# Attention projections ahead of HGRN2, in pairs, by seven products of half depth, and x kept split in DRAM

## The chip, the cores and the metric

The kernel runs on one core of one Trainium2 chip. The metric is device time in microseconds (us) of one execution, as a median of several runs. PE (TensorE) multiplies matrices, DVE (VectorE), ACT (ScalarE) and POOL (GpSimd) work on rows, and SP (SyncE) issues every DMA of this kernel, in one queue.

## The reference

One layer mixes two kinds of heads. The input (4096 rows, 1024 columns, float32) is normalised and projected to 4096 columns; half of them feed eight attention heads with three dilations, half feed four heads of a gated recurrence (HGRN2). Both results are normalised per head, gated, and projected back.

```python
hn = _rmsnorm(x, mix_norm_w[layer])
proj = hn @ w_in[layer]
aq, ak, av, ag, hq, hf, hi, hg = jnp.split(proj, split_at, axis=-1)
aq, ak = rotary(aq), rotary(ak)
attn = _longnet_mixture(bhse(aq), bhse(ak), bhse(av))
f = lb + (1.0 - lb) * jax.nn.sigmoid(hf.astype(f32))
rec = _hgrn2_chunked(silu(hq), 1.0 - f, hi, jnp.log(f))
y_attn = _head_rmsnorm(attn, attn_out_norm_w[layer], ATTN_HEADS) * silu(ag)
y_hgrn = _head_rmsnorm(rec, hgrn_out_norm_w[layer], HGRN_HEADS) * silu(hg)
x = x + jnp.concatenate([y_attn, y_hgrn], axis=-1) @ w_out[layer]
return _rmsnorm(x, final_norm_w)
```

## The kernel before

The 4096 projected columns are eight groups of 512: A0 to A3 (q, k, v and gate of two attention heads each) and H0 to H3 (one HGRN2 head each). The rows are 32 blocks of 128. Every float32 operand of a projection is split into a high part (rounded to float32r) and a low rest, so each of the eight depth steps of 128 takes three matmuls: high by high (L195), high by low (L196), low by high (L197). One block of one group is 24 matmuls of 128x512 in `project`.

The program has four stages. First, A0 to A2 are projected block by block, and `attn_rows` (L273) turns each product into rotated, transposed and split q and k (to `qk_d`), v (`v_d`) and the gate (`sg_d`), all in DRAM. Second, A3 is projected alone (L705 on). Third come the four HGRN2 groups, in 16 pairs of blocks: `load_pair` (L200) loads four raw tiles of x from xP (256 KB each) and splits them (ACT L209, POOL L210), `project_T` and `project_N` make 96 matmuls of 128x256 (L220), and `hgrn_gates`, `hgrn_values` and `hgrn_block` do the recurrence. Fourth come the output projection and the last norm (L751 on).

Attention itself is a generator in `queue`; after each block of stages two and three `take` draws as many of its steps as `rate` gives. It starts in stage two, at block `HOLD`, so it runs beside 155 blocks. Its scores, flips and weighted sums use PE, DVE and ACT; its q, k and v come by DMA (`load_qk` L406, `vh` L534 and L539).

Weights come by `load_w` (L161): 256 KB of raw weights, then the high part on ACT (L171) and the low part on DVE (L172), into eight `whi` and eight `wlo` tiles. From A3 on, raw weights and raw x share a pool of three `raw` tiles. The order on each engine is fixed when the program is built, by the framework's scheduler from the program order, priorities and its own estimates; each engine then runs its list in order, and SP too issues its DMAs in order, each after the semaphores it waits on.

```python
rate = NH * HEAD_COST / (5 * NB - HOLD)
...
            if b >= HOLD:
                left = take(left + rate)
```

Of the kernel before, what the change touches and what calls it, by code (L numbers as in the profile page):

```python
# [49 lines left out]
def layer(ctx: ExitStack, tc: tile.TileContext, x, xT, xP, pos, w_in, w_out, nw, anw, hnw, lbraw, fnw,  # L50
# [40 lines left out]
    def rotary_tables():  # L91
        su = p1p
        pt = su.tile([128, NB], I32, name="pt", bufs=1)
        pf = su.tile([128, NB], F32, name="pf", bufs=1)
# [19 lines left out]
        A.activation(rsin, ang, AF.Sin)  # L114
        A.activation(rcos, kk, AF.Sin)
# [45 lines left out]
    def load_w(g, wp, n, rp, tag, bufs, raws=()):  # L161
        for k in range(KT):
            raw = raws[k] if k < len(raws) else fetch_w(g, k, rp, tag, bufs)
            hi = wp.tile([128, 512], F32R, name="whi", bufs=n)
            lo = wp.tile([128, 512], F32R, name="wlo", bufs=n)
            if ORDER[g][0] == "H":
                parts = ((slice(0, 128), nnwt), (slice(128, 512), nwt))
            else:
                parts = ((slice(0, 512), nwt),)
            for c, s in parts:  # L170
                A.activation(hi[:, c], raw[:, c], AF.Copy, scale=s[:, k : k + 1])  # L171
                V.scalar_tensor_tensor(lo[:, c], raw[:, c], s[:, k : k + 1], hi[:, c].bitcast(F32),  # L172
                                       op0=ALU.mult, op1=ALU.subtract)
            yield hi, lo

    def load_x(b, lo_eng):
        res = []
        with tc.high_priority():
            for h in range(2):
                raw = xp.tile([128, 512], F32, name="raw", bufs=3)  # L180
                dma(raw, xT[b, :, h * 512 : (h + 1) * 512])
                hi = xp.tile([128, 512], F32R, name="xhi", bufs=4)
                lo = xp.tile([128, 512], F32R, name="xlo", bufs=4)
                A.activation(hi, raw, AF.Copy)  # L184
                lo_eng.tensor_tensor(lo, raw, hi.bitcast(F32), op=ALU.subtract)  # L185
                res.append((hi, lo))
        return res
# [12 lines left out]
    def load_pair(t):  # L200

        res = []
        with tc.high_priority():
            for q in range(4):
                raw = xp.tile([128, 512], F32, name="raw", bufs=3)
                dma(raw, xP[t, :, q * 512 : (q + 1) * 512])
                hi = xp.tile([128, 512], F32R, name="xhi", bufs=4)
                lo = xp.tile([128, 512], F32R, name="xlo", bufs=4)
                A.activation(hi, raw, AF.Copy)  # L209
                G.tensor_tensor(lo, raw, hi.bitcast(F32), op=ALU.subtract)  # L210
# [666 lines left out]
```

## Time and profile before

| | before |
|---|---|
| median of 3 runs | 2761.05 us (2759.09 to 2762.15) |
| profiled execution | 2761.07 us |
| its span | 2759.3 us |
| mean granted TensorE clock | 0.983 |
| PE busy | 2662.0 us (96%) |
| DVE, ACT, POOL busy | 1813.9, 1749.5, 997.0 us |
| DMA | 387.95 MB, mean 141 GB/s |

Busy time is the sum of an engine's instructions in the profiled execution; the span runs from its first to its last instruction. Stages lie at about 0 to 600 us (A0 to A2), 600 to 840 (A3), 840 to 2440 (HGRN2) and 2440 to the end.

### The profile page before, as it was taken

The numbers are of one execution on the slowest core, as the hardware profiler recorded it, in microseconds if no ns is written. First come the engines' busy times: TensorE is split into PE (matmuls) and PEld (weight loads), VectorE is DVE, ScalarE is ACT, GpSimd is POOL, SyncE is SP. The second block draws the span as 40 slices with busy tenths as digits, with TensorE's granted clock in tenths as the row PEclk, the third lists the DMA queues.
The fourth block names the chain that finished last, engine by engine and source line by source line (L and its number), as shares of the span: only waits on it lengthen the run. The fifth ranks groups of instructions, "written<-read, shape, count | busy, mean of one in ns | idle before, by whom it ended". The sixth has DMA issues, their size and how long they took to land.

```text
span 2759.3 us, 54301 instructions
## 1 busy us (share of the span) xinstructions
PE 2662.0 (96%) x17714; PEld 2392.6 (87%) x17714; DVE 1813.9 (66%) x5636; ACT 1749.5 (63%) x5174; POOL 997.0 (36%) x1034
## 2 busy tenths in 40 slices
PE   7999999999998999989999999999899999999998
PEld 5888888877888999988999999999899998888887
DVE  5444444445777778777778888878877878843343
ACT  6444444446766886876887787787787788422222
POOL 2222222234445535525535535544534643200000
PEclk9999999999999999989999999999999999999999
DMA  6444444476467345336435446435435533644442
GB/s 218 144 140 141 140 141 141 138 206 191 144 189 202 93 131 161 104 108 171 113 111 161 117 120 172 126 97 157 135 100 157 146 92 99 190 139 132 136 131 87
DMA packets 450189, 387.95 MB, mean 141 GB/s; under 512 B 119112, under 2 KB 342644, under 8 KB 449908
## 3 DMA queue, kind: packets, MB, share of 16 engines
q1 hardware_dynamic: 449908, 384.50, 49.3%
q8 instruction: 141, 2.31, 0.3%
q14 instruction: 140, 1.15, 0.1%
HBM read 291.53 MB, written 92.82 MB: 139 GB/s over the span
## 4 chain that ended last, share of the span: by engine, by line
PE 78%; DVE 9%; DMA 5%; ACT 4%; issue 2%; SPq 1%; POOL 1%; DVEq 0%; POOLq 0%; ACTq 0%
PE proj L220 20%; PE proj L197 12%; PE proj L195 12%; PE proj L196 12%; PE po L466 6%; PE att L454 5%; PE att L431 3%; PE att L432 3%; PE hp L369 1%; PE hp L769 1%; DVE hgv L394 1%; PE hp L373 1%; PE hp L375 1%; PE hp L380 1%; DMA wraw<-w_in 1%
## 5 line engine op out<-in xcount | busy, mean ns | idle before, releaser
L195 PE MATMUL proj<-whi,xhi 128*128 128x512 f32 x1280 | 511.4, 400 | 18.4 <-ACT rt L276 7.7
L197 PE MATMUL proj<-whi,xlo 128*128 128x512 f32 x1280 | 514.8, 402 | 0.0
L196 PE MATMUL proj<-wlo,xhi 128*128 128x512 f32 x1280 | 511.3, 399 | 0.9 <-DVE wlo L172 0.9
L210 POOL TENSOR_TENSOR xlo<-raw,xhi 128x512 fp32r<-128x512 f32 x256 | 342.6, 1343 | 229.9 <-ACT xhi L209 196.8
L442 DVE CUSTOM_DVE_ANT_0 pt<-att,mask 128x256 f32<-128x256 f32 (+1 forms) x768 | 270.3, 388 | 94.2 <-PE att L432 91.1
L220 PE MATMUL proj<-xhi,whi 128*128 128x256 f32 x1024 | 301.8, 295 | 5.7 <-DVE hz L328 2.2
L195 PEld LDWEIGHTS proj<-whi,xhi 128*128 128x128 f32 x1280 | 243.2, 190 | 70.8 <-ACT rt L276 9.6
L220 PE MATMUL proj<-xhi,wlo 128*128 128x256 f32 x1024 | 301.5, 294 | 1.6 <-DVE wlo L172 1.5
L220 PE MATMUL proj<-xlo,whi 128*128 128x256 f32 x1024 | 301.4, 294 | 0.0
L220 PE MATMUL proj<-whi,xlo 128*128 128x256 f32 x1024 | 297.9, 291 | 0.0
L220 PE MATMUL proj<-whi,xhi 128*128 128x256 f32 x1024 | 297.5, 290 | 0.3 <-ACT hgv L355 0.3
L220 PE MATMUL proj<-wlo,xhi 128*128 128x256 f32 x1024 | 296.8, 290 | 0.0
L196 PEld LDWEIGHTS proj<-wlo,xhi 128*128 128x128 f32 x1280 | 242.6, 190 | 54.6 <-DVE wlo L172 3.0
L197 PEld LDWEIGHTS proj<-whi,xlo 128*128 128x128 f32 x1280 | 242.7, 190 | 48.8
L458 DVE TENSOR_TENSOR pl<-att,ph 128x512 fp32r<-128x512 f32 (+1 forms) x384 | 238.9, 625 | 50.3 <-ACT ph L457 48.2
L444 ACT ACTIVATE pt<-pt,ml 128x256 f32<-128x256 f32 (+1 forms) x512 | 238.2, 467 | 49.1 <-DVE ml L442 47.7
L185 POOL TENSOR_TENSOR xlo<-raw,xhi 128x512 fp32r<-128x512 f32 x126 | 162.6, 1292 | 212.4 <-ACT xhi L184 188.3
L281 DVE SCALAR_TENSOR_TENSOR rot<-rt,rsin 128x32 f32<-128x32 f32 x128 | 56.5, 442 | 276.0 <-ACT rt L276 276.0
L457 ACT ACTIVATE ph<-att 128x512 fp32r<-128x512 f32 (+1 forms) x384 | 207.5, 543 | 37.6 <-PE att L454 32.0
L454 PE MATMUL att<-ident,pt 128*128 128x128 f32 x1368 | 224.7, 278 | 3.1 <-DVE nat L442 1.2
L466 PE MATMUL po<-ph,vh 128*128 128x128 f32 (+1 forms) x856 | 217.0, 278 | 9.0 <-DVE OA L552 3.5
L466 PE MATMUL po<-pl,vh 128*128 128x128 f32 (+1 forms) x856 | 212.3, 290 | 2.8 <-DVE pl L458 2.3
(210 smaller groups left out, 7228.8 us busy)
## 6 DMA issues: line engine op xcount, KB each, us to landing
raw<-xP SPq DMA_DIRECT2D x256, 256.0 KB
raw<-xT SPq DMA_DIRECT2D x128, 256.0 KB
qk_d<-stk SPq DMA_DIRECT2D x128, 256.0 KB
vh<-v_d SPq DMA_DIRECT2D x512, 64.0 KB
raw<-x SPq DMA_DIRECT2D x64, 256.0 KB
v_d<-hl SPq DMA_DIRECT2D x128, 128.0 KB
vh<-v_d SPq DMA_DIRECT2D x64, 256.0 KB
raw<-y_d SPq DMA_DIRECT2D x64, 256.0 KB
```

The costliest lines, as they stand in the source:

```text
L185: lo_eng.tensor_tensor(lo, raw, hi.bitcast(F32), op=ALU.subtract)
L195: T.matmul(ps, hi[:, c], whi, start=(k == 0), stop=False)
L196: T.matmul(ps, hi[:, c], wlo, start=False, stop=False)
L197: T.matmul(ps, lo[:, c], whi, start=False, stop=(k == KT - 1))
L210: G.tensor_tensor(lo, raw, hi.bitcast(F32), op=ALU.subtract)
L220: m = T.matmul(o, l, r, start=first is None, stop=(k == KT - 1 and g == len(groups) - 1 and n == 2))
L442: V.tensor_tensor_reduce(out=p_, in0=o, in1=mask[:, (1, 4, 16).index(d), 256 - 128 * nk : 256], scale=-0.125, scalar=3e38, op0=ALU.add, op ...
L444: A.activation(p_, p_, AF.Exp, scale=-1.0, bias=m, accum_out=l)
L454: T.transpose(ps[:, n * 128 : (n + 1) * 128], loc[u], ident)
L457: A.activation(ph[:, :w], ps[:, :w], AF.Copy)
L458: V.tensor_sub(pl[:, :w], ps[:, :w], ph[:, :w].bitcast(F32))
L466: T.matmul(po[:, 128 * c : 128 * (c + n)], v, rh, start=(s == 0), stop=(s == len(steps) - 1))
```

## The change

A0 to A3 are all projected before HGRN2, in two pairs of groups (P = 0: A0 and A1; P = 1: A2 and A3), and in units of two blocks. For a unit the product is seen as a 2x2 matrix of 2x2: rows of two blocks (first index of A), depth in two halves (second index of A, first of B), columns of two groups (second index of B). Instead of eight products of half depth, seven are made (Winograd's form of Strassen's scheme): A11·B11, S2·T2, A12·B21, S1·T1, S3·T3, S4·B22, A22·T4, where the S are sums of parts of x and the T sums of parts of the weights. Each product is 12 matmuls of 128x512 (`half`). A12·B21 is accumulated in the bank of A11·B11, and A22·T4 in that of S3·T3; `unit_rows` adds the rest on DVE.

`summed_w` makes the sums of the weights once a pair: for each of four depth steps, four raw tiles, scaled on ACT and DVE, four sums on POOL (L675, L677, L680, L683 of the changed kernel), and five splits into `tw` tiles. `load_unit` does the like for x: four tiles from xT, sums on POOL (L698, L700, L706) and DVE, seven splits (`split_tile`; ACT for the high part, L170, and DVE or POOL for the low one, L171). `attn_rows` now handles two groups of a block at once.

Attention no longer runs beside A3: its generator is drawn beside the 128 blocks of HGRN2 alone. Split x of HGRN2 is written to DRAM (`xh_d`, 512 KB a tile) by the first HGRN2 group (L197); the other three groups load it back (L200) instead of loading and splitting raw x.

```diff
+    xh_d = [dram.tile([4, 128, 1024], F32, name=f"xh_d{t}") for t in range(NB // 2)]
...
-    def load_pair(t):
+    def load_pair(t, g):
 
         res = []
         with tc.high_priority():
             for q in range(4):
-                raw = xp.tile([128, 512], F32, name="raw", bufs=3)
-                dma(raw, xP[t, :, q * 512 : (q + 1) * 512])
-                hi = xp.tile([128, 512], F32R, name="xhi", bufs=4)
-                lo = xp.tile([128, 512], F32R, name="xlo", bufs=4)
-                A.activation(hi, raw, AF.Copy)
-                G.tensor_tensor(lo, raw, hi.bitcast(F32), op=ALU.subtract)
-                res.append((hi, lo))
+                if g == 4:
+                    raw = xp.tile([128, 512], F32, name="raw", bufs=3)
+                    dma(raw, xP[t, :, q * 512 : (q + 1) * 512])
+                    xs = split_tile(raw, G, xp, "xs", 4)
+                    dma(xh_d[t][q], xs.bitcast(F32))
+                else:
+                    xs = xp.tile([128, 1024], F32R, name="xs", bufs=4)
+                    dma(xs.bitcast(F32), xh_d[t][q])
+                res.append(parts(xs))
...
+    psq = ExitStack()
+    ps_m = psq.enter_context(tc.tile_pool(name="ps_m", bufs=5, space=PSUM))
+    ps_x = psq.enter_context(tc.tile_pool(name="ps_x", bufs=3, space=PSUM))
+    w1 = one.enter_context(tc.tile_pool(name="w1", bufs=20))
+
+    def plain_w(P, j):
+
+        res = []
+        for k in range(4):
+            raw = fetch_w(2 * P, 4 * j + k, xp, "raw", 3)
+            hi = wp.tile([128, 512], F32R, name="whi", bufs=8)
+            lo = wp.tile([128, 512], F32R, name="wlo", bufs=8)
+            s = nwt[:, 4 * j + k : 4 * j + k + 1]
+            A.activation(hi, raw, AF.Copy, scale=s)
+            V.scalar_tensor_tensor(lo, raw, s, hi.bitcast(F32), op0=ALU.mult, op1=ALU.subtract)
+            res.append((hi, lo))
+        return res
+
+    def summed_w(P, W):
+        W.update({n: [None] * 4 for n in ("T1", "T2", "T3", "T4", "B22")})
+        for k in range(4):
+            B = {}
+            for j, n in ((0, 1), (0, 0), (1, 1), (1, 0)):
+                r = B[j, n] = fetch_w(2 * P + n, 4 * j + k, p1p, "xr", 5)
+                s = nwt[:, 4 * j + k : 4 * j + k + 1]
+                if n:
+                    A.activation(r, r, AF.Copy, scale=s)
+                else:
+                    V.tensor_scalar(r, r, s, None, op0=ALU.mult)
+
+            def unit(name, src, eng):
+                W[name][k] = parts(split_tile(src, eng, w1, "tw", 20))
+
+            t1 = p1p.tile([128, 512], F32, name="tmp", bufs=2)
+            G.tensor_tensor(t1, B[0, 1], B[0, 0], op=ALU.subtract)
+            t2 = p1p.tile([128, 512], F32, name="tmp", bufs=2)
+            G.tensor_tensor(t2, B[1, 1], t1, op=ALU.subtract)
+            unit("T2", t2, V)
+            unit("T1", t1, V)
+            G.tensor_tensor(B[0, 1], B[1, 1], B[0, 1], op=ALU.subtract)
+            unit("T3", B[0, 1], V)
+            unit("B22", B[1, 1], V)
+            G.tensor_tensor(B[1, 0], B[1, 0], t2, op=ALU.subtract)
+            unit("T4", B[1, 0], V)
+
+    def load_unit(t):
+
+        a, X = {}, {}
+        for i, j in ((0, 0), (1, 0), (1, 1), (0, 1)):
+            a[i, j] = p1p.tile([128, 512], F32, name="xr", bufs=5)
+            dma(a[i, j], xT[2 * t + i, :, j * 512 : (j + 1) * 512])
+
+        def split(name, src, eng):
+            X[name] = parts(split_tile(src, eng, *((p1p, "ss", 4) if name[0] == "S" else (xp, "xs", 4))))
+
+        split("A11", a[0, 0], V)
+        s1 = p1p.tile([128, 512], F32, name="tmp", bufs=2)
+        G.tensor_tensor(s1, a[1, 1], a[1, 0], op=ALU.add)
+        s2 = p1p.tile([128, 512], F32, name="tmp", bufs=2)
+        G.tensor_tensor(s2, s1, a[0, 0], op=ALU.subtract)
+        split("S2", s2, V)
+        split("A12", a[0, 1], G)
+        split("S1", s1, G)
+        V.tensor_tensor(a[1, 0], a[0, 0], a[1, 0], op=ALU.subtract)
+        split("S3", a[1, 0], G)
+        G.tensor_tensor(s2, a[0, 1], s2, op=ALU.subtract)
+        split("S4", s2, G)
+        split("A22", a[1, 1], G)
+        return X
+
+    def half(ps, X, W, start=True):
+        for k in range(4):
+            c = slice(k * 128, (k + 1) * 128)
+            (hi, lo), (whi, wlo) = X, W[k]
+            T.matmul(ps, hi[:, c], whi, start=start and k == 0, stop=False, skip_group_check=not start)
+            T.matmul(ps, hi[:, c], wlo, start=False, stop=False, skip_group_check=not start)
+            T.matmul(ps, lo[:, c], whi, start=False, stop=(k == 3), skip_group_check=not start)
+
+    def first_product(X, W):
+        pa = ps_m.tile([128, 512], F32, name="m")
+        half(pa, X["A11"], W["B11"])
+        u2 = p1p.tile([128, 512], F32, name="u2", bufs=1)
+        A.activation(u2, pa, AF.Copy)
+        return pa, u2
+
+    def unit_rows(P, t, X, W, gv, begun):
+        pa, u2 = begun
+        b0, b1 = 2 * t, 2 * t + 1
+        C0 = p1p.tile([128, 2, 512], F32, name="C", bufs=3)
+        C1 = p1p.tile([128, 2, 512], F32, name="C", bufs=3)
+        pb = ps_m.tile([128, 512], F32, name="m")
+        half(pb, X["S2"], W["T2"])
+        V.tensor_tensor(u2, pb, u2, op=ALU.add)
+        half(pa, X["A12"], W["B21"], start=False)
+        A.activation(C0[:, 0], pa, AF.Copy, scale=rstd[:, b0 : b0 + 1])
+        pc = ps_m.tile([128, 512], F32, name="m")
+        half(pc, X["S1"], W["T1"])
+        u4 = p1p.tile([128, 512], F32, name="u4", bufs=1)
+        V.tensor_tensor(u4, pc, u2, op=ALU.add)
+        pd = ps_m.tile([128, 512], F32, name="m")
+        half(pd, X["S3"], W["T3"])
+        V.tensor_tensor(C1[:, 1], pd, u4, op=ALU.add)
+        pe = ps_m.tile([128, 512], F32, name="m")
+        half(pe, X["S4"], W["B22"])
+        V.tensor_tensor(C0[:, 1], pe, u4, op=ALU.add)
+        A.activation(C0[:, 1], C0[:, 1], AF.Copy, scale=rstd[:, b0 : b0 + 1])
+        half(pd, X["A22"], W["T4"], start=False)
+        V.tensor_tensor(C1[:, 0], pd, u2, op=ALU.add)
+        A.activation(C1, C1, AF.Copy, scale=rstd[:, b1 : b1 + 1])
+        attn_rows(P, b0, C0, gv)
+        attn_rows(P, b1, C1, gv)
...
+    for P in range(2):
+        if P:
+            W = {"B11": plain_w(1, 0), "B21": plain_w(1, 1)}
...
+        summed_w(P, W)
+        for t in range(NB // 2):
+            if not P:
+                row_stats(t)
+            if P or t:
+                begun = first_product(X, W)
+            Xn = load_unit((t + 1) % (NB // 2)) if (P, t) != (1, NB // 2 - 1) else None
+            unit_rows(P, t, X, W, gv, begun)
+            X = Xn
...
-    HOLD = 5
-    rate = NH * HEAD_COST / (5 * NB - HOLD)
+    rate = NH * HEAD_COST / (4 * NB)
     left = 0.0
-    W = list(load_w(3, wp, 8, xp, "raw", 3))
-    X = load_x(0, G)
...
-        for b in range(NB):
-            Xn = load_x(b + 1, G) if b + 1 < NB else None
-            attn_rows(p1b, 3, b, project(X, W), gv3, ps_h.tile([128, 256], F32, name="hp1"))
-            X = Xn
-            if b < 4:
-                next(queue[0])
-            if b >= HOLD:
-                left = take(left + rate)
...
-    W = list(load_w(4, wp, 8, xp, "raw", 3))
-    X = load_pair(0)
+    X = load_pair(0, 4)
+    W = list(load_w(4))
+    for _ in range(4):
+        next(queue[0])
...
-                X = load_pair((t + 1) % (NB // 2))
+                X = load_pair((t + 1) % (NB // 2), g + (t + 1) // (NB // 2))
```

The first place is the start of POOL's list. The names: `xlo` is the low part of x, `ang`, `kk`, `wrap` and `rsin` belong to the rotary tables, `hl` to v; `xr` are raw tiles of x and weights, `tmp` sums. Before:

```order
L185 TENSOR_TENSOR xlo<-raw,xhi 128x512 x2
L102 TENSOR_TENSOR ang<-pf,inv 128x256
L104 TENSOR_SCALAR kk<-ang 128x256
L105 TENSOR_SCALAR kk<-kk 128x256
L109 TENSOR_SCALAR kk<-ang 128x256
```

Now, just after the rotary tables:

```order
L107 TENSOR_SCALAR rsin_105<-rsin_105 128x32x8
L105 TENSOR_SCALAR C_179<-C_179 128x256
L675 TENSOR_TENSOR tmp_257<-xr_245,xr_248 128x512
L677 TENSOR_TENSOR tmp_259<-xr_251,tmp_257 128x512
L680 TENSOR_TENSOR xr_245<-xr_251,xr_245 128x512
L683 TENSOR_TENSOR xr_254<-xr_254,tmp_259 128x512
L675 TENSOR_TENSOR tmp_290<-xr_278,xr_281 128x512
L677 TENSOR_TENSOR tmp_292<-xr_284,tmp_290 128x512
```

Before, POOL had only splits and tables there; now four such chains of four sums stand in a row, and the sums for the second unit of x follow them.

The second place is POOL at the switch from the first pair to the second (nothing like it was there before; `ss` are splits of sums of x, `C` a projected block):

```order
L171 TENSOR_TENSOR ss_3712<-tmp_3696,ss_3712 128x512
L277 TENSOR_TENSOR hl_3810<-C_3718,hl_3810 128x4x64
L677 TENSOR_TENSOR tmp_3925<-xr_3917,tmp_3923 128x512
L683 TENSOR_TENSOR xr_3920<-xr_3920,tmp_3925 128x512
L675 TENSOR_TENSOR tmp_3956<-xr_3944,xr_3947 128x512
L277 TENSOR_TENSOR hl_3838<-C_3719,hl_3838 128x4x64
L677 TENSOR_TENSOR tmp_3958<-xr_3950,tmp_3956 128x512
L680 TENSOR_TENSOR xr_3944<-xr_3950,xr_3944 128x512
L683 TENSOR_TENSOR xr_3953<-xr_3953,tmp_3958 128x512
```

The chain of the first depth step mixes with the last unit's rows; those of the other three follow in a row.

The third place is SP's list inside a later HGRN2 group, where q, k and v of a coming head are also loaded (`KH`, `KL`, `QS`, `vh`; `hrb` is a row of norms, `y_d` and `sgt` belong to the end of a head). Before:

```order
L206 DMA raw_17094<-xP 128x512
L325 DMA hrb_17015<-rstd_d_84 128x256
L206 DMA raw_17100<-xP 128x512
L206 DMA raw_17106<-xP 128x512
L206 DMA raw_17112<-xP 128x512
L539 DMA vh_16345<-v_d1_77 128x4x128
L206 DMA raw_17457<-xP 128x512
```

Now:

```order
L314 DMA hrb_19162<-rstd_d_88 128x256
L528 DMA vh_16376<-v_d1_65 128x4x128
L200 DMA xs_18848<-xh_d14_82 128x1024
L200 DMA xs_18850<-xh_d14_82 128x1024
L395 DMA QS_7125<-qk_d1_61 64x512
L396 DMA QS_7125<-qk_d1_61 64x512
L200 DMA xs_18852<-xh_d14_82 128x1024
L200 DMA xs_18854<-xh_d14_82 128x1024
L395 DMA KH_7126<-qk_d1_61 64x512
```

Where raw tiles of 128x512 came ahead of their splits, split tiles of 128x1024 come straight into the four `xs` tiles that the matmuls read, each after the matmuls of the pair before have left it.

More of the change, by code (lines that the diff above doesn't have):

```diff
@@ new lines, in attn_rows @@
+        t2 = p1p.tile([128, 2, 4, 16], F32, name="rot")
+        c = C[:, :, 0:256].rearrange("p g (q e) -> p g q e", q=4)
+        for n in range(2):
+            sn = rsin[:, b : b + 1, 8 * n : 8 * n + 8].unsqueeze(1).to_broadcast([128, 2, 4, 8])
+            V.tensor_mul(t2[:, :, :, 8 * n : 8 * n + 8], c[:, :, :, 8 - 8 * n : 16 - 8 * n], sn)
+        c16 = c[:, :, :, 0:16]
+        V.tensor_mul(c16, c16, rcos[:, b : b + 1, :].unsqueeze(1).to_broadcast([128, 2, 4, 16]))
+        V.tensor_add(c16, c16, t2)
@@ new lines, in attn_rows @@
+        hl = p1p.tile([128, 2, 2, 128], F32R, name="hl")
+        rv = C[:, :, 256:384].rearrange("p g (q e) -> p g q e", q=2)
+        V.tensor_copy(hl[:, :, :, 0:64], rv)
+        G.tensor_tensor(hl[:, :, :, 64:128], rv, hl[:, :, :, 0:64].bitcast(F32), op=ALU.subtract)
+        for g in range(2):
+            dma(v_d[2 * P + g][bs], hl[:, g].bitcast(F32))
+        pt_ = ps_x.tile([128, 512], F32, name="tr")
+        for g in range(2):
+            for q in range(2):
+                T.transpose(pt_[:, g * 256 + q * 128 : g * 256 + (q + 1) * 128], C[:, g, q * 128 : (q + 1) * 128], ident)
@@ L301, in attn_rows @@
+        st = p1p.tile([128, 2, 4, 128], F32R, name="stk")
+        p4 = pt_.rearrange("p (g n c) -> p g n c", g=2, n=2)
+        A.activation(st[:, :, 0:2], p4, AF.Copy)
+        V.tensor_sub(st[:, :, 2:4], p4, st[:, :, 0:2].bitcast(F32))
+        for g in range(2):
+            dma(qk_d[2 * P + g][:, :, bs], st[:, g].bitcast(F32))
+        e = p1p.tile([128, 2, 128], F32, name="sg")
+        A.activation(e, C[:, :, 384:512], AF.Exp, scale=-1.0)
         sigm(e)
-        V.tensor_mul(e, e, rt[:, 384:512])
+        V.tensor_mul(e, e, C[:, :, 384:512])
@@ L661, in layer @@
+    W = {"B11": plain_w(0, 0)}
+    X = load_unit(0)
+    rotary_tables()
+    W["B21"] = plain_w(0, 1)
+    begun = first_product(X, W)
     constants()
-    gv = [load_vec(p1p, n) for n in ORDER[:3]]
     tc.strict_bb_all_engine_barrier()
     A.preload_act_table_set("natural_log_exp_and_others")
-    def rows(g, b, ps):
-        attn_rows(p1p, g, b, ps, gv[g], ps_t.tile([128, 256], F32, name="att"))
-    with tc.high_priority():
-        row_stats(0)
-    rows(0, 0, ps0)
-    for g in range(3):
-        if g:
-            W4[g] = list(load_w(g, w1, 16, p1p, "wraw", 4, raws if g == 1 else ()))
-            rows(g, 0, project(X, W4[g]))
-        ps0 = project(X1, W4[g])
-        if g == 0:
-            row_sums(1)
-            row_stats(1)
-        rows(g, 1, ps0)
@@ L747, in layer @@
         if g < 7:
[L748 removed]
+            W = list(load_w(g + 1))
     def fetch_wo(n, k, rp, tag, bufs):
```

176 lines of the change are left out of this document (59 added, 117 removed).

## The prediction

> **What bounds the kernel now.** I read the page's busy table first, then the chain that ended last, then the busy time by stretches of the span.
>
> ```profile
> PE 2662.0 (96%) x17714; PEld 2392.6 (87%) x17714; DVE 1813.9 (66%) x5636; ACT 1749.5 (63%) x5174; POOL 997.0 (36%) x1034
> PE 78%; DVE 9%; DMA 5%; ACT 4%; issue 2%; SPq 1%; POOL 1%; DVEq 0%; POOLq 0%; ACTq 0%
> ```
>
> TensorE is busy for 2662 us and is 78% of the chain. The other 22% must sit in a few places, since 2759.3 − 2662.0 leaves only 97 us idle. The stretches show where (columns: window, length, then busy us and instruction count of PE, PEld, DVE, ACT, POOL, then granted clock, DMA share, GB/s):
>
> ```profile
> 0.00:20.00 20.00, 9.53 (x24) 5.32 (x24) 10.77 (x17) 12.74 (x20) 9.90 (x14) 1.00 0.83 272
> 20.00:40.00 20.00, 15.52 (x52) 11.92 (x53) 12.96 (x44) 14.86 (x33) 0.92 (x1) 0.83 0.76 233
> 80.00:580.00 500.00, 500.00 (x2247) 403.58 (x2246) 212.18 (x970) 239.20 (x657) 111.68 (x142) 1.00 0.47 140
> 600.00:620.00 20.00, 16.31 (x72) 12.24 (x71) 6.25 (x22) 7.01 (x17) 6.34 (x7) 1.00 1.07 275
> 620.00:640.00 20.00, 16.09 (x61) 12.39 (x60) 6.03 (x16) 5.13 (x12) 7.05 (x8) 0.83 1.03 248
> 640.00:840.00 200.00, 197.94 (x1137) 170.15 (x1136) 145.90 (x492) 146.14 (x419) 84.04 (x89) 0.99 0.59 173
> 840.00:860.00 20.00, 12.11 (x58) 10.12 (x56) 15.82 (x53) 14.33 (x40) 4.55 (x5) 0.77 0.74 211
> 890.00:1190.00 300.00, 294.75 (x2485) 286.02 (x2483) 239.34 (x716) 242.72 (x756) 152.45 (x158) 1.00 0.45 122
> 1190.00:1290.00 100.00, 86.00 (x621) 79.01 (x620) 72.91 (x213) 69.61 (x208) 32.34 (x30) 0.89 0.58 152
> 1570.00:1670.00 100.00, 96.03 (x791) 92.05 (x790) 80.74 (x245) 86.55 (x264) 37.43 (x41) 0.98 0.48 128
> 1940.00:2040.00 100.00, 91.08 (x704) 86.80 (x703) 78.43 (x233) 76.97 (x237) 48.68 (x51) 0.93 0.47 126
> ```
>
> The attention projections (80 to 580 us) leave PE no gap. The losses are the start, the first q/k loads (600 to 640), the first HGRN2 pair (840 to 860), and the three switches of HGRN2 group. A steady stretch issues 2485/300 = 8.28 instructions per us; the three switch windows hold 2116 where 2484 would fit, 368 × 0.12 = 44 us lost. What a matmul costs is read from starts in the chain:
>
> ```profile
> 299.97 0.23 PE proj L196
> 300.20 0.24 PE proj L197
> 300.44 0.24 PE proj L195
> ```
>
> Two steps take 0.47 us, so 0.235 us for one 128x512 matmul (the 400 ns of the groups overlap their neighbours). In the stretch 80 to 580, 26 instructions (24 matmuls and two transposes) take 26 × 500/2247 = 5.79 us.
>
> **Part 1: the products.** Per pair of groups and unit of two blocks, seven products of 12 matmuls replace 96: 84. Over 2 × 16 units that is 384 matmuls fewer, all in work that PE alone bounds: 384 × 0.235 = **−90 us**. The Trainium skill, "TensorE: Matmul & The Clock Gate", section "Back-to-back issue gap", gives about 216 ns for 512 columns; by it, as an estimate, the saving would be 83 us. The rows here have 0.235, and they decide.
>
> **Part 2: the start.** Before, 24 matmuls run in the first 20 us and 52 in the next, where the full rate is 2247/500 × 20 = 90: (66 + 38)/90 × 20 = 23 us lost. After, every weight row k needs a serial cycle, because its first raw tile waits for the buffer that T3 of row k−1 frees: load, scale on DVE, three sums on POOL, two halves of a split. Prices from these rows (a chain piece, then groups):
>
> ```profile
> 23.98 4.04 DMA wraw<-w_in
> ...
> L185 POOL TENSOR_TENSOR xlo<-raw,xhi 128x512 fp32r<-128x512 f32 x126 | 162.6, 1292 | 212.4 <-ACT xhi L184 188.3
> ...
> L209 ACT ACTIVATE xhi<-raw 128x512 fp32r<-128x512 f32 x256 | 158.6, 622 | 25.1 <-DMA raw<-xP 10.3 <-PE proj L220 8.8 <-issue 4.4
> L458 DVE TENSOR_TENSOR pl<-att,ph 128x512 fp32r<-128x512 f32 (+1 forms) x384 | 238.9, 625 | 50.3 <-ACT ph L457 48.2
> ```
>
> 4.04 + 0.63 + 3 × 1.29 + 0.62 + 0.63 = 9.8 us, four times 39 us, behind a barrier at some 28 us (in the trace it ends near 21; more loads and sums now stand ahead of it). PE has only a few whole products that need no sum: I count 96 matmuls, 22.5 us, by 70 us. Loss 48, so **+25**; bounds +10 (the loads of the next row overlap the sums better) and +40 (the second unit's sums stand behind the weights' on POOL).
>
> **Part 3: a new switch between the pairs.** The same four chains stand on POOL once more at mid-phase, row 0 mixed with the last unit's sums, three in a row, 3 × 9.8 = 29 us. With two splits of the next unit's x between them, some 3 us, that is 32, and PE has the last unit (84 matmuls, 20 us) and two plain products (24 matmuls, 5.6 us) as cover: 6 left. DVE and ACT serve the last unit's rows at the same time, so I take **+13**; bounds 5 (only one chain uncovered) and 30 (no cover).
>
> **Part 4: moved transitions.** The third group's weight phase disappears with A3's own stage: 600 to 640 lost 7.6 us and 840 to 860 another 7.9. Now the q/k loads, the first x pair and its writes to DRAM coincide at one transition, where DMA stood at 1.03 to 1.07 of its engines with loads alone. I put 10 us there: 10 − 15.5 is about **−6**; bounds −15 and +10.
>
> **Part 5: the switches of HGRN2 group.** The chain through the first one, where raw tiles of x and w share three buffers:
>
> ```profile
> 1248.25 3.61 DMA raw<-w_in
> ...
> 1262.02 2.51 DVE wlo L172 x2
> 1266.81 5.21 DMA raw<-xP
> 1272.74 1.30 POOL xlo L210
> 1274.06 5.78 DMA raw<-xP
> ```
>
> With x reloaded already split, three weight tiles can wait ready and no POOL split stands in this chain; but the eight split tiles still come free only with the last product of the group, so five loads stay serial. Of 44 us I take off **−12**; bounds −40 and 0.
>
> **Part 6: the reload.** For 48 pairs four 512 KB tiles replace four 256 KB raw tiles and their splits. What is saved is not on the path (ACT 622 ns and POOL 1343 ns, L210, beside a full PE). What is risked is: before, raw tiles were prefetched and only the split (0.62 + 1.34 us) lay between a freed tile and its next use; now the load does. The instruction order has about 7 us of PE work there, tile by tile. The chain above shows 5.21 and 5.78 us for 256 KB, issue to landing, at a crowded moment. Four tiles a pair at the 275 GB/s of the crowded stretch above take 7.6 us. So most pairs just make it and some, beside q/k loads, come late. Two things wait then: on SP, the load of a tile stands until PE frees it, and behind it stand the v and q/k loads that attention's matmuls need; on PE, the attention work that follows in the fixed order stands behind the first L220 matmul, and DVE and ACT starve after it. I take 0.3 us a pair, **+15**; bounds 0, and 2 us each, +96.
>
> **Part 7: denser attention.** Attention had 155 block slots and has 128, each with 21% more of it. PE's share only moves, but DVE and ACT, at 239 and 243 of 300 us, go up: per block by the row at 890, 8.8 of 11.1 us for DVE, to about 9.9 of 11.8. PE lost 1.8% there; I add **+8** over 1500 us; bounds −10 (ACT and POOL are freed of x splits) and +40.
>
> **Part 8: in-order stalls in the new units.** A unit is 20.3 us on PE; I count 11 to 15 us on ACT, 13 on DVE and 12 on POOL. A product's bank is copied before its next use with about 29 matmuls, 6.8 us, between. **+5**; bounds 0 and +40.
>
> Sum: −90 + 25 + 13 − 6 − 12 + 15 + 8 + 5 = −42. The profiled execution took 2761.07 (span 2759.3), the median is 2761.05, so no shift between them: about **2720 us**.
>
> **Rivals.**
> - **A, slower: the reload is late.** Its place is the wait of a pair's first L220 matmul on a DMA. If 512 KB takes twice the 5.2 us, 10.4, against 7 of cover, about 3 us are lost in 45 pairs: +135 in place of +15, **2840**. It decides the sign from (90 − 25 − 13 + 6 + 12 − 8 − 5)/48 = 1.2 us a pair. For: the two pieces above and one queue for all transfers. Against: DMA at 0.45 in steady stretches. Chance 0.16.
> - **B: queueing under denser attention.** DVE at over 84% with an in-order partner; +40 for +8: **2752**. Against: PE at 98% in the stretch with DVE at 80%. Chance 0.12.
> - **C: more relief.** Start and pair switch at their lower bounds, switches cut by 30, no late reload: −15 − 8 − 18 − 15, **2664**. Chance 0.12.
> - **D: the change doesn't do what it says.** The unit takes what four plain blocks took, 4 × 5.79 = 23.2 us, because row work or sums on DVE and POOL bound it: the −90 is gone, **2810**. Against: no engine over 15 of 20 us by my count. Chance 0.05.
> - **E: the reload is always covered.** 256 KB took 4.04 us where 0.95 is its share at 275 GB/s, so 3.1 go by whatever the size; 512 KB would land in 3.1 + 1.9 = 5.0 us, under the 7 of cover: 0 for +15, **2705**. Against: 5.2 and 5.8 us for half the bytes. Chance 0.15. The Trainium skill, "DMA: Bandwidth & Descriptors", section "Anatomy of one DMA — SWDGE (gpsimd) path", fits 2.0 us plus the bytes at 436 GB/s, for another issuing path than this one; as an estimate that is 3.2 us for 512 KB, and it would give the same 2705.
>
> **How the numbers follow.** The forecast, 2720, has 0.40; its own range is 2690 to 2745. The range that should hold 8 in 10 takes in C's 2664, E, B, and 0.04 of A, loads late by up to 1.7 us a pair (2705 + 82 = 2787): **2660 to 2790**; what is left out is 0.12 of A, D, and 0.03 below C. A change within 0.2%, 5.5 us, is about what a measurement can't tell from none. Faster: the forecast, C, E and 0.07 of B, 0.74; same: the rest of B, 0.05, and 0.01 of A near its break-even, 0.06; slower: the other 0.15 of A, and D, 0.20.
>
> **What would show it.** Part 1: in the new phase PE busy over 98%, 84 matmuls and eight transposes in 20.3 us. Parts 2 and 3: two gaps of PE, at 30 to 70 us and near mid-phase, released by POOL or splits of the tw tiles. Part 6: idle before L220 released by the DMA of xs; above 1.2 us a pair it is rival A. Part 5: more than 2116 instructions around the three switches. Part 7: PE busy below 98% in steady stretches, released by DVE, means B. I am wrong if units last longer than 22 us or if the gaps at the two weight phases exceed 80 us together.

## The result and the profile after

The changed kernel takes 2821.2 us (median of 4 runs, 2819.4 to 2826.0) beside 2760.96 for the one before: ratio 1.0222, 95% interval 1.0204 to 1.0239. It is **slower by 60 us**, where 42 us faster was forecast. The profiled execution has a span of 2820.3 us and a mean granted TensorE clock of 0.961 (before 0.983).

The page's busy table and the chain after:

```profile
PE 2610.1 (93%) x17330; PEld 2345.8 (83%) x17330; DVE 1955.0 (69%) x5242; ACT 1693.5 (60%) x4831; POOL 973.6 (35%) x941
PE 62%; DMA 9%; DVE 4%; ACT 3%; SPq 2%; issue 1%; POOL 1%; DVEq 0%; POOLq 0%; ACTq 0%
```

PE has 384 matmuls fewer and is busy 52 us less, but the span grew by 61: PE's idle time went from 97 to 210 us. The stretches show where (columns as in the prediction):

```profile
0.00:100.00 100.00, 47.63 (x134) 33.39 (x135) 64.97 (x100) 57.98 (x130) 55.92 (x49) 0.73 0.57 182
100.00:200.00 100.00, 87.81 (x383) 70.07 (x382) 84.48 (x199) 68.75 (x182) 54.28 (x44) 0.97 0.76 230
200.00:400.00 200.00, 200.00 (x920) 165.34 (x919) 153.39 (x260) 104.71 (x192) 125.64 (x100) 1.00 0.48 147
400.00:500.00 100.00, 78.33 (x304) 58.67 (x303) 80.22 (x116) 51.53 (x95) 63.89 (x48) 0.86 0.51 154
760.00:880.00 120.00, 99.56 (x725) 93.61 (x724) 57.74 (x172) 69.57 (x198) 46.74 (x48) 0.89 0.83 249
780.00:2230.00 1450.00, 1399.02 (x11615) 1351.10 (x11613) 1055.63 (x3325) 1046.61 (x3292) 458.74 (x522) 0.99 0.65 190
2230.00:2440.00 210.00, 152.79 (x929) 129.82 (x929) 141.83 (x484) 127.26 (x405) 43.46 (x44) 0.83 0.40 110
```

A full stretch (200 to 400) issues 4.6 instructions per us. The first 200 us hold 134 + 383 where 920 would fit: (920 − 517)/4.6 = 88 us lost, where the kernel before lost 23. The switch of pairs (400 to 500) loses (460 − 304)/4.6 = 34 us. And there is a tail that the forecast did not have at all: from 2230 to 2440 PE runs at a clock of 0.83 and is idle for 57 of 210 us.

What runs there is seen in the first and last starts of two matmuls: one of each HGRN2 block's transposes, and the scores of attention. Of the changed kernel (count, then shortest, median and longest duration in ns, then first and last start in us):

```profile
L355 PE MATMUL hp<-ident,hkd x128: 270/272/477, 791.9 to 2232.1; 128*128 128x128 f32 x128
L420 PE MATMUL att<-KH,QS x256: 220/283/582, 943.9 to 2434.2; 128*128 128x256 f32 x120, 128*128 128x128 f32 x8
```

The same two of the kernel before:

```profile
L366 PE MATMUL hp<-ident,hkd x128: 270/272/421, 882.6 to 2347.6; 128*128 128x128 f32 x128
L431 PE MATMUL att<-KH,QS x256: 221/283/582, 769.5 to 2374.2; 128*128 128x256 f32 x120, 128*128 128x128 f32 x8
```

Before, HGRN2's last block and attention's last score are 27 us apart; now 202. HGRN2 is done early, and 120 of the 768 scores are left behind it and run alone. The static order of PE has the same: behind the last HGRN2 projection stand 128 score matmuls of each kind (KH, KL), where before stood 10. In the changed kernel `rate` asks for 768/128 = 6 scores a block, but the scheduler's order has about five, as many as the kernel before was asked for (768/155).

### The profile page after: what moved, and what is told of

Its sections match the earlier page's. It is cut to its first block, busy times and chain, and to the rows that moved or that the text cites. A ratio compares the mean times of both kernels' runs of the same rounds, so it can differ in the third digit from the quotient of the medians.

```text
span 2820.3 us, 52045 instructions
## 1 busy us (share of the span) xinstructions
PE 2610.1 (93%) x17330; PEld 2345.8 (83%) x17330; DVE 1955.0 (69%) x5242; ACT 1693.5 (60%) x4831; POOL 973.6 (35%) x941
## 4 chain that ended last, share of the span: by engine, by line
PE 62%; DMA 9%; DVE 4%; ACT 3%; SPq 2%; issue 1%; POOL 1%; DVEq 0%; POOLq 0%; ACTq 0%
PE proj L210 18%; PE po L455 5%; PE proj L183 4%; PE proj L185 4%; PE proj L184 4%; DMA xs<-xh_d 4%; PE att L443 4%; PE att L420 3%; PE m L715 3%; PE m L717 3%; PE m L716 3%; PE att L421 3%; ACT pt L433 1%; PE hp L850 1%; PE hp L358 1%
## 5 line engine op out<-in xcount | busy, mean ns | idle before, releaser
L210 PE MATMUL proj<-xs,whi 128*128 128x256 f32 x2048 | 435.9, 297 | 36.2 <-DMA xs<-xh_d 22.1
L210 PE MATMUL proj<-whi,xs 128*128 128x256 f32 x2048 | 427.5, 290 | 5.7 <-DVE hz L317 5.7
L210 PEld LDWEIGHTS proj<-xs,whi 128*128 128x128 f32 x2048 | 333.7, 194 | 51.0 <-DMA xs<-xh_d 24.7
L210 PEld LDWEIGHTS proj<-whi,xs 128*128 128x128 f32 x2048 | 333.0, 191 | 7.2 <-DVE hz L317 6.0
L210 PE MATMUL proj<-xs,wlo 128*128 128x256 f32 x1024 | 301.0, 294 | 0.0
L210 PE MATMUL proj<-wlo,xs 128*128 128x256 f32 x1024 | 296.4, 289 | 0.0
L715 PE MATMUL m<-tw,ss 128*128 128x512 f32 x512 | 205.2, 405 | 21.9 <-ACT tw L170 21.8
L716 PE MATMUL m<-tw,ss 128*128 128x512 f32 x512 | 206.9, 404 | 4.0 <-DVE tw L171 4.0
L717 PE MATMUL m<-tw,ss 128*128 128x512 f32 x512 | 207.4, 405 | 1.6 <-DVE ss L171 1.6
L210 PEld LDWEIGHTS proj<-xs,wlo 128*128 128x128 f32 x1024 | 198.8, 194 | 1.2 <-issue 1.0
L210 PEld LDWEIGHTS proj<-wlo,xs 128*128 128x128 f32 x1024 | 196.1, 191 | 0.6 <-issue 0.5
L455 PEld LDWEIGHTS po<-ph,vh 128*128 128x128 f32 x856 | 166.2, 194 | 19.4 <-ACT ph L446 7.4
L443 PEld LDWEIGHTS att<-ident,pt 128*128 128x128 f32 x1368 | 163.2, 144 | 12.3 <-ACT pt L433 4.8
```

What stands on the lines that cost most here:

```text
L210: m = T.matmul(o, l, r, start=first is None, stop=(k == KT - 1 and g == len(groups) - 1 and n == 2))
L443: T.transpose(ps[:, n * 128 : (n + 1) * 128], loc[u], ident)
L455: T.matmul(po[:, 128 * c : 128 * (c + n)], v, rh, start=(s == 0), stop=(s == len(steps) - 1))
L715: T.matmul(ps, hi[:, c], whi, start=start and k == 0, stop=False, skip_group_check=not start)
L716: T.matmul(ps, hi[:, c], wlo, start=False, stop=False, skip_group_check=not start)
L717: T.matmul(ps, lo[:, c], whi, start=False, stop=(k == 3), skip_group_check=not start)
```

## The experiments

Ratios are to the kernel before on the same chip; a ratio of 1.002 is 5.5 us. Kernels that ran on different chips are compared by the difference of their ratios.

**One part of the change alone.** Three kernels take the change apart. The first is the kernel before with attention drawn beside HGRN2 only:

```diff
-    rate = NH * HEAD_COST / (5 * NB - HOLD)
+    rate = NH * HEAD_COST / (4 * NB)
...
-            if b >= HOLD:
-                left = take(left + rate)
```

> The kernel before with one thing changed: attention is drawn only beside the 128 blocks of HGRN2, not beside A3 (no products of half depth, no reload). Theory T (the leftover): attention runs at about 5 scores a block beside HGRN2 whatever the rate asks, so about 114 of 768 scores are left behind the last HGRN2 projection and run alone, at a half idle PE: 70 to 100 us more than before, 2830 to 2860 us. Rival (the tail belongs to the reload or to the new units): within 10 us of before, 2750 to 2775.

Measured: 2813.3 us, 1.0201 (1.0183 to 1.0219), **+57 us** by the medians, 55 by the ratio. So the late attention alone costs nearly as much as the whole change, though somewhat less than the 70 us expected. (Only 14 scores of the first head still run beside A3, where the kernel before has 94.) Its tail is the changed kernel's:

```profile
L366 PE MATMUL hp<-ident,hkd x128: 269/272/421, 810.9 to 2231.8; 128*128 128x128 f32 x128
L431 PE MATMUL att<-KH,QS x256: 223/283/582, 902.0 to 2426.5; 128*128 128x256 f32 x120, 128*128 128x128 f32 x8
```

HGRN2 ends at the same 2232 as in the changed kernel, with 114 scores left. The second is the kernel before with the reload alone (`load_pair` of the changed kernel, `xs` tiles in place of `xhi` and `xlo`):

> The kernel before with the stored and reloaded split x alone. If the reload is covered and relieves the switches of HGRN2 group (as the trace of the changed kernel has it: 26 us lost around the switches where there were 60), 15 to 35 us less than before: 2726 to 2746. If reloads come late (the forecast's case A), more than before: above 2765.

Measured: 2736.8 us, 0.9925 (0.9902 to 0.9949), **19 us faster**, as expected. The three switches of HGRN2 group, which lost 44 us before, are nearly full: 843, 848 and 789 instructions where 621, 791 and 704 stood. The switches come some 40 us earlier in this kernel, and so do its windows; each lies about the first product of a new group as it does in the kernel before:

```profile
1150.00:1250.00 100.00, 99.81 (x843) 97.00 (x842) 77.11 (x243) 84.07 (x264) 27.55 (x35) 1.00 0.69 211
1528.00:1628.00 100.00, 100.00 (x848) 97.16 (x847) 77.24 (x258) 80.40 (x260) 30.83 (x41) 1.00 0.58 170
1895.00:1995.00 100.00, 94.67 (x789) 90.73 (x788) 78.96 (x236) 69.00 (x221) 33.96 (x38) 0.99 0.73 206
```

The third is the changed kernel without the reload:

```diff
-                if g == 4:
+                if True:
                     raw = xp.tile([128, 512], F32, name="raw", bufs=3)
                     dma(raw, xP[t, :, q * 512 : (q + 1) * 512])
                     xs = split_tile(raw, G, xp, "xs", 4)
-                    dma(xh_d[t][q], xs.bitcast(F32))
```

> The changed kernel with raw x loaded and split for all four HGRN2 groups, nothing stored. If the reload saves at the switches and costs nothing in the pairs, 15 to 40 us more than the changed kernel: 2836 to 2861; if the late loads cost more than the switches gain, less than it: below 2815.

Measured: 2827.6 us, 1.0253 (1.0233 to 1.0273), 9 us above the changed kernel by the ratios (6 by the medians): less than the 15 expected, of the expected sign, and the two intervals overlap a little. This kernel differs from the first of the three by the products of half depth and what comes with them: 1.0253 against 1.0201, so **the products, with their start and switch, cost 14 us instead of gaining**.

**Putting the tail back beside HGRN2.** Two ways. First by an order on PE: the first projection matmul of a pair stands behind the last score drawn two pairs before.

```diff
+                        if hold is not None:
+                            after(m, hold)
...
-            qd, kd, ea = hgrn_gates(t, project_T(X, W))
+            qd, kd, ea = hgrn_gates(t, project_T(X, W, marks[-2]))
...
+            marks.append(hst.get("m"))
```

> The changed kernel, with an order on PE alone: the first projection matmul of an HGRN2 pair stands behind the last score drawn two pairs before. 4 scores instead of 120 are left behind the last projection. Theory T: the work of the tail moves beside HGRN2 and most of the 106 us lost there come back, 60 to 95 us less than the changed kernel: 2725 to 2760. Rival (DVE and ACT cannot carry more attention a block, the forecast's case B): HGRN2 blocks stretch by as much as the tail shrinks, 2800 to 2840.

Measured: 2808.3 us, 1.0184 (1.0166 to 1.0202). The tail is gone, and only 10 us come back by the ratios (13 by the medians): that lies within the rival's 2800 to 2840, and far from the 60 to 95 us of theory T. HGRN2's stage has stretched: PE idles there for 99 of 1625 us (766 to 2391), where the changed kernel has 51 of 1450 (780 to 2230). Second, by PSUM banks: in the order, two banks for attention leave 344 scores behind the last block, three leave 120, four leave 2, while four to six `pt` buffers (VectorE's copies of the scores) change nothing. So three banks set attention's pace in the order.

```diff
-    ps_p = ctx.enter_context(tc.tile_pool(name="ps_p", bufs=2, space=PSUM))
-    ps_t = ctx.enter_context(tc.tile_pool(name="ps_t", bufs=3, space=PSUM))
+    ps_p = ctx.enter_context(tc.tile_pool(name="ps_p", bufs=1, space=PSUM))
+    ps_t = ctx.enter_context(tc.tile_pool(name="ps_t", bufs=4, space=PSUM))
```

> The changed kernel with four PSUM banks for attention's scores, flips and transposes instead of three, and one for HGRN2's projections instead of two. In the order 2 scores are left behind the last projection instead of 120. Theory T2 (attention's three banks set its pace beside HGRN2, and the tail is what that pace leaves over): the tail's 106 us go, the single projection bank costs about 0.3 to 0.7 us a pair, 2740 to 2780. Rival (more attention a block cannot be carried, as the order forced on PE alone gave back 13 us only): 2800 to 2830.

Measured: 2823.3 us, 1.0243 (1.0228 to 1.0258): nothing gained. But the edit had a price elsewhere, seen in the output projection, which also uses `ps_p`. Of this kernel, and of the changed one:

```profile
2500.00:2800.00 300.00, 281.13 (x1273) 224.00 (x1271) 111.51 (x249) 68.13 (x180) 0.00 (x0) 1.00 0.37 113
```

```profile
2500.00:2800.00 300.00, 300.00 (x1426) 250.68 (x1426) 121.21 (x276) 69.54 (x202) 0.00 (x0) 1.00 0.43 129
```

With one bank PE does 153 instructions fewer in 300 us. So the output projection got attention's four banks in the next run (`project` takes its tile from `ps_t`):

> The changed kernel with four attention banks and one bank for HGRN2's projections, and the output projection taking its banks from attention's four (in the run with one bank the output stage lost 10 us in each 100 where it loses 1 otherwise). If that alone hid the gain, some 35 us less than that run: 2783 to 2795, so a third to a half of the late attention's price is given back by a denser order. If density gives nothing back, 2810 to 2825.

Measured: 2795.8 us, 1.0136 (1.0118 to 1.0155), 24 us below the changed kernel's ratio, just past the expected window. Its HGRN2 stage and its scores:

```profile
780.00:2370.00 1590.00, 1510.96 (x12444) 1450.19 (x12443) 1174.35 (x3754) 1155.67 (x3651) 495.38 (x560) 0.98 0.64 184
```

```profile
L355 PE MATMUL hp<-ident,hkd x128: 270/272/457, 790.6 to 2373.3; 128*128 128x128 f32 x128
L420 PE MATMUL att<-KH,QS x256: 222/283/562, 924.8 to 2385.4; 128*128 128x256 f32 x120, 128*128 128x128 f32 x8
```

The 118 scores that moved cost 1583 − 1440 = 143 us beside HGRN2, 1.2 us each, with the price of the single projection bank in it; alone in the tail they took 202/120 = 1.7. PE idles for 79 of 1590 us in this stage where the changed kernel idles for 51 of 1450. So about 24 of the 55 us of late attention are the tail's order, and some 31 stay when the order is dense, again with the single bank's price. Whether VectorE's queue is behind these was tried by moving three of its operations to GpSimd:

```diff
-        V.scalar_tensor_tensor(kd, e[:, 0], omlb, cum, op0=ALU.mult, op1=ALU.mult)
+        G.tensor_scalar(cum, cum, omlb, None, op0=ALU.mult)
+        G.tensor_tensor(kd, e[:, 0], cum, op=ALU.mult)
...
-            V.tensor_scalar(sp, st["R"], st["g"], g, op0=ALU.mult, op1=ALU.mult)
+            G.tensor_scalar(sp, st["R"], st["g"], g, op0=ALU.mult, op1=ALU.mult)
```

(and the gated output, L394 of the kernel before, in two operations of GpSimd)

> As the run before, with three VectorE operations of HGRN2 (kd L343, the scaled state L379, the gated output L394; some 170 us of VectorE in the kernel before) moved to GpSimd, which has room. If VectorE's queue is what makes dense attention cost PE time: 15 to 40 us less than the run before. If it is the length of the chains, or GpSimd's slower operation on HGRN2's own chain counts, equal or up to 40 us more.

Measured: 2796.5 us, 1.0142 (1.0116 to 1.0168), no difference. From 780 to 2365 us VectorE is busy for 113 us less than in the run before (1056 where it was 1169), and PE idles for 73 us where it idled for 77. So a lighter VectorE alone does not free the dense order; that GpSimd's longer operations gave back a gain is not excluded. Whether the length of attention's chains or the single projection bank holds it, stays open.

**The opposite of the change in one respect.** The kernel before, with A2 as well projected alone beside attention, so that attention has 187 blocks instead of 155:

```diff
-    rate = NH * HEAD_COST / (5 * NB - HOLD)
+    rate = NH * HEAD_COST / (6 * NB - HOLD)
...
+        for g in (2, 3):
+            if g == 3:
+                W = list(load_w(3, wp, 8, xp, "raw", 3))
...
-            if b >= HOLD:
-                left = take(left + rate)
+                if g == 3 or b >= HOLD:
+                    left = take(left + rate)
```

> The kernel before with A2 also projected alone beside attention: attention has 187 blocks, not 155 (the opposite of the change in this one respect). If the room that attention is given is what counts, 10 to 30 us less than before (2728 to 2748 against 2758), since the last head ends with HGRN2 and the switches find less to do; if only the leftover behind HGRN2 counts, which before hardly had, within 8 us of before, or up to 15 more for one more weight phase.

Measured: 2730.8 us, 0.9912 (0.9895 to 0.9928), **25 us faster**. The room given to attention counts in both directions: 27 blocks fewer cost 57 us, 32 more gain 25 (with one more stage of a single group in it). With the reload added:

> The kernel before with A2 beside attention as well (187 blocks) and with x of HGRN2 stored split and reloaded. If the two gains (25 and 19 us) come from different places they add: 2706 to 2718. If both relieve the same switches of HGRN2 group: 2722 to 2735.

Measured: 2715.2 us, 0.9843 (0.9823 to 0.9864): the gains add, and this kernel **beats both**. With the three operations on GpSimd on top:

> The first kernel of this call with the same three operations on GpSimd: there PE waits some 32 us for VectorE in the stretch 900 to 2200. 5 to 20 us less than the first if VectorE's queue is the cause, equal or up to 40 us more if GpSimd's latency is on the chain.

Measured: 2719.7 us, 0.9860 (0.9840 to 0.9879), the same within the intervals.

**The start and the switch.** First, an order: the row sums' loads behind the unit's own loads on SP, and one raw weight tile of four in the `raw` tiles.

```diff
-            dma(a[i, j], xT[2 * t + i, :, j * 512 : (j + 1) * 512])
+            hst["x", t] = dma(a[i, j], xT[2 * t + i, :, j * 512 : (j + 1) * 512])
...
-                dma(xr, x[(2 * t + i) * 128 : (2 * t + i + 1) * 128, h * 512 : (h + 1) * 512])
+                after(dma(xr, x[(2 * t + i) * 128 : (2 * t + i + 1) * 128, h * 512 : (h + 1) * 512]), hst["x", t])
...
-                r = B[j, n] = fetch_w(2 * P + n, 4 * j + k, p1p, "xr", 5)
+                r = B[j, n] = fetch_w(2 * P + n, 4 * j + k, *((xp, "raw", 3) if (j, n) == (1, 0) else (p1p, "xr", 5)))
```

> The changed kernel with two things at the weight phases: row sums' loads of x stand behind the same unit's xT loads in SP's list, and one of the four raw weight tiles a depth step goes into the idle raw tiles, so that the loads of a step no longer wait for the step before. If SP's list and the five xr tiles set the 10 to 11 us a depth step, the start loses some 60 instead of 87 us and the switch 20 to 25 instead of 35: 2780 to 2795. If POOL's four sums and the splits set it, within 10 us of the changed kernel: 2811 to 2825.

Measured: 2827.7 us, 1.0264 (1.0246 to 1.0281): slower, where a gain or nothing was expected. A depth step took 7.6 us on average instead of 9.6, and the first 100 us hold 172 matmuls instead of 134; but the next 200 give that back, and the units behind them are slower too. Of this kernel, then of the changed one:

```profile
100.00:300.00 200.00, 180.05 (x803) 143.36 (x803) 135.19 (x304) 113.40 (x257) 106.58 (x86) 0.99 0.55 173
230.00:420.00 190.00, 172.10 (x765) 137.13 (x764) 127.02 (x267) 106.58 (x232) 107.98 (x85) 0.99 0.56 174
```

```profile
100.00:300.00 200.00, 187.81 (x843) 152.73 (x842) 161.50 (x329) 120.40 (x277) 118.00 (x94) 0.98 0.62 188
230.00:420.00 190.00, 183.75 (x837) 150.52 (x835) 149.71 (x250) 103.43 (x191) 118.44 (x94) 0.99 0.50 152
```

From 230 to 420 PE waits there for 12.3 us on VectorE's sum into `C` (L742), for which the changed kernel does not wait at all. The likely cause is the new place of the row sums, since the other edit, the raw tile, gained by itself in a kernel without row sums (the last of this section); the new place alone was not tried. One more kernel had both these edits and the banks of the second way above (four for attention, one for projections). It was expected at 2700 to 2740 us if the two costs were separate and both theories held; measured are 2849.0 us, 1.0336 (1.0320 to 1.0352), the slowest of all, some 26 us above the banks alone by the ratios. Of these, 9 us stand before HGRN2, whose first product starts at 776.2 instead of 766.9 us, and 16 within it; why the second part is there was not traced.

So the parts were taken away one at a time. Without POOL's four sums of the weights:

```diff
-            G.tensor_tensor(t1, B[0, 1], B[0, 0], op=ALU.subtract)
-            G.tensor_tensor(t2, B[1, 1], t1, op=ALU.subtract)
+            t1 = B[0, 0]
+            t2 = B[0, 1]
...
-            G.tensor_tensor(B[0, 1], B[1, 1], B[0, 1], op=ALU.subtract)
...
-            G.tensor_tensor(B[1, 0], B[1, 0], t2, op=ALU.subtract)
```

> The changed kernel without POOL's four sums of the weights per depth step (the T are then plain tiles: loads, scales, splits and products stay). If the sums are what makes a depth step take 10 to 11 us at the start, the start loses some 20 us less (87 to about 67) and the switch some 10 to 15 less: 2785 to 2795. If loads and SP's list set the step, within 10 us of the changed kernel: 2811 to 2825.

Measured: 2782.1 us, 1.0078 (1.0054 to 1.0102), **40 us** off the changed kernel by the ratios. Its start and switch:

```profile
0.00:100.00 100.00, 62.60 (x220) 44.58 (x220) 67.38 (x126) 66.04 (x149) 45.97 (x42) 0.85 0.66 211
...
400.00:500.00 100.00, 90.46 (x387) 71.75 (x388) 81.67 (x140) 55.05 (x105) 56.01 (x44) 0.95 0.51 157
```

(220 − 134)/4.6 = 19 us at the start, (387 − 304)/4.6 = 18 at the switch. Without the row sums of all units but the first:

```diff
     def row_stats(t):

+        if t:
+            V.tensor_copy(rstd[:, 2 * t : 2 * t + 2], rstd[:, 0:2])
+            return
```

> The changed kernel with the row sums (loads of x, squares, inverse roots) of all units but the first left out, the first one's values used for all. If their loads on SP's list ahead of weight loads, and their work on ACT, are a part of the start's loss: 20 to 40 us less, 2780 to 2800, nothing at the switch. If the weights' own chain sets the start: within 8 us of the changed kernel.

Measured: 2790.8 us, 1.0124 (1.0109 to 1.0139), **27 us** off by the ratios. And with the one raw tile of four moved besides:

> As the run before, with one of the four raw weight tiles of a depth step in the then idle raw tiles. If the five xr tiles hold the next step's loads back: another 10 to 20 us at the start and 5 to 10 at the switch less; if POOL's sums and the splits set the step, within 6 us of the run before.

Measured: 2781.8 us, 1.0086 (1.0063 to 1.0109), another 9 us by the medians, between the two expectations: more than the 6 of the second, short of the 15 at least that five tiles holding the loads back would have given. The start of the kernel without row sums, its raw tiles unmoved:

```profile
0.00:100.00 100.00, 53.66 (x165) 38.38 (x166) 62.39 (x98) 47.78 (x86) 60.91 (x52) 0.76 0.41 137
100.00:200.00 100.00, 98.03 (x443) 80.17 (x442) 78.66 (x137) 49.89 (x93) 65.43 (x51) 0.98 0.48 147
```

Row sums cost the start (608 − 517)/4.6 = 20 us, most of it from 100 to 200, where the first units work; the depth steps hardly change without them (6.7, 10.5 and 10.3 us). Both parts count, the sums at both places and the row sums at the first: the time from PE's 1400th instruction to its 1800th, in which the switch lies, is 123 us in the changed kernel, 107 without the sums and 122 without the row sums.

## Why the prediction was wrong

The forecast was −42 us and the result +60. Its steps, one by one:

- **Part 7, denser attention, failed as a step.** It said that attention has 128 slots and that each holds 21% more, for +8, with +40 as the bound. The order does not give each slot more: attention keeps its pace of about five scores a block, and the sixth part that does not fit runs behind HGRN2. Measured by itself it costs 57 us (1.0201), and even in an order that fits it all, some 31 by the difference of ratios, of which the single projection bank may be a part. The moved places of attention's instructions could be read from the order before any run; the part had argued from busy shares alone. Case B named queueing under denser attention, at +40, the nearest of the rivals, but put its place inside HGRN2's blocks; in the changed kernel it is behind them.
- **Part 2, the start: right in kind, mis-sized.** +25 was forecast, 88 − 23 = 65 measured. The depth steps took 6.7, 10.7 and 11.3 us, 9.6 on average where 9.8 was forecast each; as they spread so far about it, that the mean fits is in part luck (starts of the first sum of a step, on POOL):

```profile
37.09 1.27 POOL L675 TENSOR_TENSOR tmp<-xr 128x512 f32<-128x512 f32 x1 [7.39 <-DVE xr L669]
...
43.77 1.60 POOL L675 TENSOR_TENSOR tmp<-xr 128x512 f32<-128x512 f32 x1 [1.09 <-ACT tw L170]
...
54.48 1.60 POOL L675 TENSOR_TENSOR tmp<-xr 128x512 f32<-128x512 f32 x1 [2.79 <-DVE tw L171]
...
65.75 1.57 POOL L675 TENSOR_TENSOR tmp<-xr 128x512 f32<-128x512 f32 x1 [1.73 <-ACT raw L252]
```

  What the sum missed is the work of PE in front of them and the time behind them:

```profile
0.00:70.00 70.00, 26.70 (x60) 17.34 (x60) 41.08 (x57) 38.52 (x81) 37.24 (x34) 0.69 0.53 169
70.00:100.00 30.00, 20.93 (x75) 16.05 (x75) 23.89 (x43) 19.46 (x49) 18.67 (x15) 0.82 0.66 213
```

  By 70 us PE has done 60 matmuls where the forecast counted 96, so 70 − 60/4.6 = 57 us are lost there instead of 48. Behind 70 us the forecast put no loss at all, and there 75 + 383 instructions run where 130 × 4.6 = 598 would fit: another 30 us. Row sums are 20 us of the start's loss by the run without them (ACT raw L252 is one); the rest is not taken apart, with the first units' own splits after 75 us and a clock of 0.73 in the first 100 us as what stands there.
- **Part 3, the switch: mis-sized.** +13 forecast (5 to 30), 34 measured; the sums are over half of it (18 us). The gaps at the two weight phases are 88 + 34 = 122 us together, above the 80 that the forecast had named as its sign of being wrong.
- **Parts 1 and 8, the units: right.** 92 instructions (84 matmuls and eight transposes) in 200/920 × 92 = 20.0 us, 20.3 forecast. Against 4 × 5.79 = 23.2 that is −3.2 × 32 = −101 us, where the parts together had −85. The stalls of part 8 did not come. Case D is out.
- **Part 5, switches of group: the sign right, the size past its bound.** −12 forecast with −40 as the bound, since five loads were to stay serial. With the reload alone the three windows hold 2480 instructions instead of 2116: 364 × 0.12 = 44 us, all that was lost there. In the changed kernel less came through. The same three windows of the changed kernel without the reload, then of the changed kernel:

```profile
1080.00:1180.00 100.00, 98.52 (x831) 95.36 (x830) 82.53 (x244) 88.08 (x270) 39.35 (x42) 1.00 0.47 131
1461.00:1561.00 100.00, 95.52 (x786) 91.62 (x785) 83.93 (x252) 86.32 (x271) 47.83 (x52) 0.98 0.44 121
1823.00:1923.00 100.00, 95.55 (x776) 90.50 (x775) 81.87 (x222) 73.07 (x214) 59.84 (x57) 0.98 0.59 165
```

```profile
1076.00:1176.00 100.00, 99.75 (x846) 97.30 (x846) 82.83 (x265) 86.72 (x275) 31.63 (x38) 1.00 0.62 189
1456.00:1556.00 100.00, 98.72 (x838) 96.12 (x838) 80.15 (x263) 78.00 (x252) 33.18 (x41) 1.00 0.63 185
1828.00:1928.00 100.00, 94.36 (x793) 91.33 (x792) 80.32 (x241) 69.43 (x219) 37.05 (x39) 1.00 0.77 220
```

  They hold 2393 and 2477: with attention late the switches lose less even without the reload (2306 in the kernel with late attention alone), so it finds only 84 × 0.12 = 10 us there.
- **Part 6, the reload: right.** +15 forecast. What waited for the reloads in the changed kernel, under that line's DMA issues (us, times):

```profile
  PEld proj L210: 24.7, 25
  PE proj L210: 22.1, 21
```

  22 us in 21 places, 0.46 us a pair over 48 (and 22.7 us in the kernel with the reload alone). Rival A, 3 us a pair, is refuted; the net of parts 5 and 6 was measured at −19 us by itself. Case E was too good by those 22 us.
- **Part 4, transitions: off by a little.** By PE's idle time, as the forecast counted it, 760 to 880 loses 120 − 99.6 = 20 us, and the two places before lost 7.6 + 7.9: +5 where −6 was forecast. In the chain of the changed kernel stand the writes of split x, which hold the `xs` tiles (and no load was late in that form before):

```profile
790.36 8.30 DMA raw<-xP
798.68 8.48 DMA xh_d<-xs
807.18 9.45 DMA xh_d<-xs
816.64 7.38 DMA xh_d<-xs
```

By runs, the change is late attention +2.0%, the products with their start and switch +0.5%, and the reload −0.3%, together 2.2%. By windows and single runs the pieces (−101, +65, +34, +5, +57 and −19) add to +41; the missing 19 us were not traced to one place. One part is seen: the reload gave 19 us in the kernel before and 6 to 9 in the changed one, where the switches had less to give. That does not close either: 10 us won at the switches less 22 of part 6 would be a loss, and where the rest of that gain comes from stays open.

## What to carry to other kernels

Work that fills the gaps of another stage needs room as much as rate: before moving it, count from the new order where its instructions end up, and price the leftover by itself, at the pace of a chain that runs alone. A saving of matmuls by sums of operands must be set against its preparation at each place where PE has nothing else to do; here two preparations cost as much as 32 units saved. Of a change with three parts, each part timed alone says more than the sum: here one part (the reload) was a gain, and with attention spread wider instead of narrower it gave a kernel 1.6% faster than the one before.

## What the runs showed of the hardware

In the stretches where PE idles most, the granted clock is lowest (0.73 in the first 100 us of the changed kernel, 0.83 in its tail, 0.86 at the switch, 1.00 where PE is full), and the matmuls that PE does have follow each other more slowly. In the stretch from 20 to 40 us and in three steps of it, matmuls of 128x512 start 0.43 us apart, where at a clock of 1.00 they start 0.235 us apart (at 300 us of the kernel before):

```profile
20.00:40.00 20.00, 5.46 (x12) 3.80 (x12) 4.38 (x6) 7.31 (x12) 10.93 (x13) 0.59 0.34 122
...
34.17 0.63 PE L717 MATMUL m<-whi,xs 128*128 128x512 f32 x1
34.60 0.63 PE L715 MATMUL m<-whi,xs 128*128 128x512 f32 x1
35.03 0.63 PE L716 MATMUL m<-wlo,xs 128*128 128x512 f32 x1
```

A write of 512 KB from `xs` to DRAM stood for 7.4 to 9.5 us on the chain where three stood in a row beside loads.
